# A two-layer trunk of RG-LRU and stick-breaking attention: three mask matmuls for four in each head, other shares of the last output tiles, and small moves in the half-wide unit

## The chip, the cores and the metric

The kernel runs on one core of a Trainium2 chip. The metric is the device time of one execution in microseconds (us); a kernel's time is the median of its runs. The trace was taken by the hardware profiler during one further execution, and that execution's own time is given beside its span.

Engines are named as the profile names them: PE is TensorE's matmuls, PEld its weight loads, DVE is VectorE, ACT is ScalarE, POOL is GpSimd, and SP is SyncE, which only issues transfers here.

## What is computed

The input is one sequence of 512 tokens with 1024 channels in float32. Two layers are applied, the first with an RG-LRU recurrent block, the second with stick-breaking attention of 16 heads of 64 channels; each is followed by a SwiGLU feed-forward network (FFN) of 2816 hidden channels, and a root-mean-square norm precedes each of the four. Cut to the parts that the change touches:

```python
def reference(x, norm_mix_g, norm_ffn_g, a_w_in, ...):
    for layer in range(DEPTH):
        h = _rmsnorm(x, norm_mix_g[layer])
        mix = rglru(h) if layer == 0 else _sb_mixer(h, b_w_qkv, b_w_out)
        x = x + mix
        h = _rmsnorm(x, norm_ffn_g[layer])
        x = x + (silu(h @ w_gate[layer]) * (h @ w_up[layer])) @ w_down[layer]
    return _rmsnorm(x, final_g)

def _stick_breaking_attention(q, k, v):           # one block of 128 queries
    z = (q @ k.T) / sqrt(64)
    mask = key_pos < q_pos                        # strictly causal
    log_beta = log_sigmoid(z)
    log_1m = where(mask, log_sigmoid(-z), 0.0)
    suffix = cumsum(log_1m, reverse=True) - log_1m
    wts = where(mask, exp(log_beta + suffix), 0.0)
    return wts @ v
```

## The kernel before, in words

**Precision.** Every float32 product is made of three fp32r matmuls: an operand is cast to a high part and the difference is its low part; `mm3` (L350) issues high by high, high by low, low by high (L352 to L354 in the trace). A weight tile of 128 x 1024 is loaded into `raw`, cast to `wh` (L306 on ACT, or L304 on DVE while `wh_dve` is set), and subtracted to `wl` (L307). `split_one` (L309) does this for the next tile in a fixed list, the plan. `wl_engine` (L321) chooses the engine of the subtraction: by the table `wl_on` (L191) for the tiles listed in it, else POOL for odd tiles and DVE for even ones outside the FFNs. Tiles 20 and 21 are the first two of the recurrent block's output weight `w_ao`.

**Order.** PE, ACT, DVE and POOL run their instructions in the order in which the program issues them in the FFNs and in attention, so the place of a call in the code is its place in each engine's queue. `chunk` (L329) hands out the next split weight tile and first splits ahead of it: the loop runs until `ahead` tiles beyond the one handed out are split, four in the FFNs, two elsewhere, unless an argument says otherwise.

**FFN.** The 2816 hidden channels are six units; units 0 to 4 are 512 channels wide and unit 5 (`u == NU`) 256. Each unit computes gate and up products for pairs of token blocks by seven products (`g1` to `g7`) instead of eight, and the down product in the same way (`d1` to `d7`), in an order given as a string (L56 to L64). For unit 5 it is

```python
self.order = "g5 g1 tt g6 o1 g3 o2 d1 g2 d2 g7 d6 d5 g4 q2 d7 tn d3 d4"
```

`product` (L846) takes one weight tile by `chunk` and issues its matmuls (L773 to L775 in the trace). `g3` adds bank results to the two tiles `u` (`u2_add`, L893, traced as L765). `q2` (L931) scales the two tiles `b` from two PSUM banks (L933). `tn` (L954) turns `u` and `b` by eight 128 x 128 transpositions (L780) into two banks.

**Attention.** Heads run in a software pipeline of 17 steps (L1275 to L1331). In step h, `s1(h+1)` (L1125) puts the scores of the next head into three PSUM banks: key block 0 with 512 queries in the first, key block 1 with 384 in the second, key blocks 2 and 3 with 256 and 128 in the third. Each key block takes two products (L1131, L1132) and one bf16 matmul of the identity with a mask tile (L1133), which adds −1e30 to the diagonal block of 128 columns. `chain_a` (L1138) forms softplus on ACT (Abs L1149, Exp L1150, Ln L1151), DVE and POOL; `s2` (L1175) adds the suffix sums by matmuls (L1186); `chain_b` (L1191) forms the weights' high and low parts (`awh`, `awl`, L1199 to L1201); `s3` (L1205, matmuls at L1212) multiplies them by v, and `s3_evac` (L1222) adds the result into `o` (L1225, L1226). After each second head `osplit` (L1242) forms the pair's high and low parts `oh` and `ol` (L1245, L1246).

While heads 0 to 12 run, PE has projections of later heads to fill its time. From step 13 on the fill is the output projection: `out_part(m, lo, hi)` (L1251) adds pairs lo to hi−1 into output tile m, three matmuls a pair. `out_split` splits one output weight tile with both the cast and the subtraction on DVE. Of the steps that matter here:

```python
elif h == 13: out_part(0, 0, 3, fill, 6)
elif h == 14: out_part(0, 3, 6, None, 6)
elif h == 15: osplit(6); out_part(1, 0, 6, fill)
elif h == 16: out_part(2, 0, 4, self.bank[0])
...
if h in (13, 15): out_split()        # behind s2(h) and chain_b(h), ahead of s3_evac(h - 1)
```

Behind the loop `osplit(7)` and the remaining parts of tiles 2, 1 and 0 follow.

Of the kernel before, what the change touches and what calls it, by code (L numbers as in the profile page):

```python
# [16 lines left out]
P = 128  # L17
# [153 lines left out]
class Kern:  # L171
    def __init__(self, ctx, tc, a, out):
        self.ctx, self.tc, self.nc, self.a, self.out = ctx, tc, tc.nc, a, out
        mk = lambda name, bufs, **kw: ctx.enter_context(tc.tile_pool(name=name, bufs=bufs, **kw))
        self.const = mk("const", 1)
        self.wp = mk("wp", 1)
        self.tp = mk("tp", 1)
        self.ar = mk("ar", 1)
        self.free = deque((0, i) for i in range(NS1))
        self.free2 = deque()  # L180
        self.clock = 0
        self.keep2 = 0
        self.slot = {}
        pp = mk("pp", 1, space=bass.MemoryType.PSUM)
        self.bank = [pp.tile([P, S], F32, name=f"bank{i}") for i in range(8)]
        self.bi = 0
        self.tn = 0
        self.later, self.done, self.chain = [], set(), {}
        self.wl_dve = self.wh_dve = False
        self.ring4 = None  # L190
        self.wl_on = {**dict.fromkeys((*range(5, 12), 14, 18), self.nc.gpsimd),  # L191
                      **dict.fromkeys((2, 3, 4, 12, 13, 15, 16, 17, 19), self.nc.vector)}
# [544 lines left out]
    def ffn(self, l, gnext):  # L737
# [3 lines left out]
        with tc.tile_pool(name=f"ffn{l}", bufs=1) as self.fp, \  # L741
# [96 lines left out]
            for u in range(NU + 1):  # L838
# [7 lines left out]
                def product(q, out, first=True):  # L846
                    for c in range(un.np):
                        wh, wl = self.chunk()
# [52 lines left out]
                def g3():  # L901
                    product(3, B, False)
                    u2_add()

# [49 lines left out]
                def tn():  # L954
                    turn((0, 1), A)
# [68 lines left out]
    def attention(self):  # L1024
# [5 lines left out]
        with ExitStack() as cx:  # L1030
# [6 lines left out]
            t0 = ap_.tile([P, P], F32, name="t0")  # L1037
# [3 lines left out]
            msk = ap_.tile([P, P], BF16, name="msk")  # L1041
            sp2 = [ap_.tile([P, S], F32, name="sp2")]
            for t in sp2:
# [8 lines left out]
            nc.gpsimd.affine_select(out=msk, in_=msk, compare_op=ALU.is_ge, fill=0.0,  # L1052
                                    base=0, pattern=[[-1, P]], channel_multiplier=1)
# [71 lines left out]
            def s1(h):  # L1125
                hd = heads[h]
                zt, b = zslot(h)
                for kt in range(4):
# [4 lines left out]
                    mm(zt[kt][:, 0:P], lhsT=idb, rhs=msk, start=False, stop=True, skip_group_check=True)  # L1133
# [95 lines left out]
            with tc.manual_schedule(engines={E.PE, E.Activation, E.DVE, E.Pool}):  # L1229
# [45 lines left out]
                for h in range(NH + 1):  # L1275
# [6 lines left out]
                    elif h == 13:  # L1282
                        fill = mps()
                        out_part(0, 0, 3, fill, 6)
                    elif h == 14:
                        out_part(0, 3, 6, None, 6)
# [3 lines left out]
                    elif h == 16:  # L1290
                        out_part(2, 0, 4, self.bank[0])
# [27 lines left out]
                    if h in (13, 15):  # L1319
# [9 lines left out]
                out_part(2, 4, 7)  # L1329
# [94 lines left out]
```

## Time and profile before

| | before |
|---|---|
| median of 3 runs | 1112.52 us (1112.18 to 1112.86) |
| the profiled execution's own time | 1113.21 us |
| its span in the trace | 1111.5 us, granted clock 0.997 |
| instructions | 14758 |
| DMA, mean over the span | 159.87 MB, 144 GB/s |
| mask matmuls (L1133) | 64, from 558.0 to 716.1 |

A row of the trace's timeline gives start, duration, engine, line, operation, out<-in with shapes, the count of instructions in the row, and in brackets the idle time of the engine before it and what ended it. Matmul ends are modelled and overlap the next start, so PE's pace is read from the distance of starts. A row of the windows gives the stretch, its length, then busy time and instructions of PE, PEld, DVE, ACT and POOL, then PE's granted clock, the DMA engines' share and GB/s. The lines themselves stand in the prediction.

### The profile page before, as it was taken

Reading aid. Unit: us, or ns where it says so; the run is one execution under the profiler, and the core shown is the slowest. Engines: PE = TensorE matmul, PEld = TensorE weight load, DVE = VectorE, ACT = ScalarE, POOL = GpSimd, SP = SyncE. Lnnn points to the kernel's source line nnn. Section 1 sums busy time; section 2 is a strip of 40 time slices with the busy share of each in tenths; the row PEclk is TensorE's granted clock in tenths of the full one; section 3 lists DMA queues with packets and bytes.
Section 4 is the critical chain, followed back from the end, with each engine's and each line's share of the span. In section 5 each row is a group of like instructions: output and inputs, shape, how many; then the busy total and the mean of one; then the engine's idle time right before and its main releaser. Section 6 shows DMA issues by size and latency. Waiting matters only on the chain.

```text
span 1111.5 us, 14758 instructions
## 1 busy us (share of the span) xinstructions
PE 1092.8 (98%) x5265; PEld 908.7 (82%) x5265; DVE 901.6 (81%) x1260; ACT 710.0 (64%) x1084; POOL 359.9 (32%) x251
## 2 busy tenths in 40 slices
PE   9999999999999999999999999999999999999996
PEld 6888788878888888888888888778888888888885
DVE  7878887687978888987378889968669797978897
ACT  7598567565646464535389999957765555646454
POOL 2353242324151413204043445403232424151411
PEclk9999999999999999999999999999999999999999
DMA  8512339877667765442243423224987766765421
GB/s 284 172 71 99 112 109 214 189 199 183 161 193 157 197 164 171 99 130 94 84 121 96 117 77 95 77 76 125 212 180 204 169 188 168 164 193 119 149 63 75
DMA packets 48825, 159.87 MB, mean 144 GB/s; under 512 B 6000, under 2 KB 7280, under 8 KB 48752
## 3 DMA queue, kind: packets, MB, share of 16 engines
q1 hardware_dynamic: 36368, 113.84, 29.7%
q0 software_dynamic: 12384, 45.09, 23.2%
q8 instruction: 41, 0.67, 0.2%
q14 instruction: 32, 0.26, 0.1%
HBM read 148.43 MB, written 2.10 MB: 135 GB/s over the span
## 4 chain that ended last, share of the span: by engine, by line
PE 76%; DVE 9%; ACT 3%; issue 2%; DMA 1%; POOL 0%; DVEq 0%; ACTq 0%; POOLq 0%
PE bank L773 16%; PE bank L774 16%; PE bank L775 16%; PE bank L352 7%; PE bank L354 7%; PE bank L353 7%; DVE wl L307 4%; PE bank L1186 3%; PE bank L1212 2%; DVE y L765 1%; PE bank L780 1%; DMA bu<-w_gu 1%; PE bank L1131 1%; ACT wh L306 1%; PE bank L1132 1%
## 5 line engine op out<-in xcount | busy, mean ns | idle before, releaser
L307 DVE TENSOR_TENSOR wl<-raw,wh 128x1024 fp32r<-128x1024 f32 (+1 forms) x117 | 176.4, 1511 | 37.6 <-ACT wh L306 37.4
L306 ACT CAST wh<-raw 128x1024 fp32r<-128x1024 f32 (+1 forms) x142 | 143.1, 1012 | 91.9 <-PE bank L775 38.2
L773 PE MATMUL bank<-wh,ow 128*128 128x512 f32 (+1 forms) x480 | 179.8, 375 | 1.8 <-DVE u L765 1.8
L775 PE MATMUL bank<-wh,ow 128*128 128x512 f32 (+1 forms) x480 | 178.3, 372 | 0.0
L774 PE MATMUL bank<-wl,ow 128*128 128x512 f32 (+1 forms) x480 | 178.3, 371 | 0.0
L92 POOL DMA_DIRECT2D bu<-w_gu x64 | 56.0, 876 | 270.0 <-DVE wl L307 101.4
L306 ACT CAST wh<-bu 128x1024 fp32r<-128x1024 f32 x66 | 69.4, 1053 | 65.7 <-PE bank L775 40.5
L307 DVE TENSOR_TENSOR wl<-bu,wh 128x1024 fp32r<-128x1024 f32 x66 | 80.5, 1237 | 32.6 <-ACT wh L306 31.6
L773 PEld LDWEIGHTS bank<-wh,ow 128*128 128x128 f32 x480 | 90.4, 188 | 18.3 <-DVE u L765 2.6
L775 PEld LDWEIGHTS bank<-wh,ow 128*128 128x128 f32 x480 | 90.4, 188 | 15.7
L352 PE MATMUL bank<-uh,wh 128*128 128x512 f32 x256 | 102.3, 400 | 0.8 <-ACT uh L408 0.8
L774 PEld LDWEIGHTS bank<-wl,ow 128*128 128x128 f32 x480 | 90.4, 188 | 15.4
L354 PE MATMUL bank<-uh,wl 128*128 128x512 f32 x256 | 100.1, 392 | 0.4 <-DVE wl L307 0.4
L353 PE MATMUL bank<-ul,wh 128*128 128x512 f32 x256 | 99.7, 389 | 0.3 <-DVE ul L409 0.3
L307 POOL TENSOR_TENSOR wl<-raw,wh 128x1024 fp32r<-128x1024 f32 (+1 forms) x27 | 62.1, 2301 | 101.9 <-ACT wh L306 99.4
L765 DVE TENSOR_TENSOR y<-y,bank 128x512 f32<-128x512 f32 x140 | 88.9, 679 | 2.4 <-PE bank L775 2.3
L773 PE MATMUL bank<-wh,hth 128*128 128x512 f32 x192 | 75.2, 392 | 0.1
L774 PE MATMUL bank<-wl,hth 128*128 128x512 f32 x192 | 74.8, 389 | 0.0
L775 PE MATMUL bank<-wh,htl 128*128 128x512 f32 x192 | 74.7, 389 | 0.0
L307 DVE TENSOR_TENSOR wl<-bv,wh 128x1024 fp32r<-128x1024 f32 x44 | 58.3, 1336 | 13.2 <-ACT wh L306 13.2
L1154 POOL TENSOR_TENSOR spl<-t,sph 128x512 fp32r<-128x512 f32 (+1 forms) x32 | 39.1, 1244 | 84.1 <-DVE sph L1153 81.2
L306 ACT CAST wh<-bv 128x1024 fp32r<-128x1024 f32 x44 | 46.0, 1051 | 18.1 <-PE bank L775 8.7
(258 smaller groups left out, 2778.0 us busy)
## 6 DMA issues: line engine op xcount, KB each, us to landing
bu<-w_gu POOLq DMA_DIRECT2D x64, 512.0 KB, 5.8
raw<-w_gu SPq DMA_DIRECT2D x44, 512.0 KB, 3.8
raw<-w_dn SPq DMA_DIRECT2D x24, 512.0 KB, 5.3
bu<-w_gu SPq DMA_DIRECT2D x22, 512.0 KB, 4.2
bv<-w_gu SPq DMA_DIRECT2D x22, 512.0 KB, 4.3
bv<-w_gu POOLq DMA_DIRECT2D x22, 512.0 KB, 6.2
d<-w_dn SPq DMA_DIRECT2D x20, 512.0 KB, 3.5
raw<-w_qk SPq DMA_DIRECT2D x16, 512.0 KB, 3.4
```

Of the source, the lines that this page charges most:

```text
L92: kern.soon(lambda: kern.nc.gpsimd.dma_start(t, self.part(n), accum_op=ALU.add))
L306: self.nc.scalar.copy(wh[:, c], raw[:, c])
L307: self.wl_engine(i).tensor_tensor(wl[:, c], raw[:, c], wh[:, c].bitcast(F32), ALU.subtract)
L352: mm(out, lhsT=wh, rhs=xh, start=first, stop=False)
L353: mm(out, lhsT=wh, rhs=xl, start=False, stop=False)
L354: mm(out, lhsT=wl, rhs=xh, start=False, stop=last)
L765: add = lambda o, a, b: nc.vector.tensor_tensor(o, a, b, ALU.add)
L773: mm(out, lhsT=xh, rhs=wh, start=first, stop=False, skip_group_check=True)
L774: mm(out, lhsT=xh, rhs=wl, start=False, stop=False, skip_group_check=True)
L775: mm(out, lhsT=xl, rhs=wh, start=False, stop=last, skip_group_check=True)
L1154: nc.gpsimd.tensor_tensor(sl[:, w], sp[:, w], sh[:, w].bitcast(F32), ALU.subtract)
L1186: mm(zt[kt][:, o0:o0 + ZW[j]], lhsT=tri if j == kt else one_n, rhs=s_, start=False, stop=True, skip_group_check=True)
```

## The change

- `wl_on`: tile 20's subtraction goes to POOL (tile 21's was there by the default).
- Unit 5, `g3`: `chunk(3)` splits one tile fewer ahead of g3's products; that split comes by `split_one` behind the adds of `u2_add`.
- Unit 5, `tn`: the same eight transpositions, first the four of `u`, then the four of `b`. Before, the first four went into bank 2 (two of `u`, two of `b`) and the others into bank 3; now the third and fourth turn `u` into bank 3.
- Masks: key block 0's mask stays behind its products. Those of key blocks 1 to 3 stand behind all products of the head: one of 128 columns in the second bank, one of 256 columns in the third. `msk` is 256 columns wide, made by two `affine_select` on POOL.
- Output tiles: of tile 0, step 13 does two pairs (three before) and step 14 four; of tile 2, step 16 does pairs 0 to 4 (0 to 3 before) and the tail 5 and 6.
- `out_split` of output weight tile 2 stands in step 14, not 15.
- `t0` is a temporary of the ring of six instead of a tile of its own.

```diff
--- before.py
+++ after.py
@@ -188,7 +188,7 @@
         self.later, self.done, self.chain = [], set(), {}
         self.wl_dve = self.wh_dve = False
         self.ring4 = None
-        self.wl_on = {**dict.fromkeys((*range(5, 12), 14, 18), self.nc.gpsimd),
+        self.wl_on = {**dict.fromkeys((*range(5, 12), 14, 18, 20, 21), self.nc.gpsimd),
                       **dict.fromkeys((2, 3, 4, 12, 13, 15, 16, 17, 19), self.nc.vector)}
 
     def ps(self):
@@ -845,7 +845,7 @@
 
                 def product(q, out, first=True):
                     for c in range(un.np):
-                        wh, wl = self.chunk()
+                        wh, wl = self.chunk(3 if u == NU and q == 3 else None)
                         for j in range(2):
                             for i in range(un.kt):
                                 k = c * un.kt + i
@@ -901,6 +901,8 @@
                 def g3():
                     product(3, B, False)
                     u2_add()
+                    if u == NU:
+                        self.split_one()
 
                 G = B4
 
@@ -952,7 +954,11 @@
                     operands2(1, db, self.cx)
 
                 def tn():
-                    turn((0, 1), A)
+                    for ab in (u2, b5):
+                        for f in range(2):
+                            for j in range(2):
+                                t = j + 2 * (ab is b5)
+                                nc.tensor.transpose(A[f][:, ts(t)], ab[j][:, ts(f)], self.ident)
                     for p in range(2):
                         split([t[:, p] for t in hn], A[p])
 
@@ -1034,11 +1040,11 @@
             vs = [[None] * 4 for _ in range(NT)]
             o = [None] * NP
             ou = [None] * NP
-            t0 = ap_.tile([P, P], F32, name="t0")
+            t0 = self.tmp()[:, :P]
             tri = ap_.tile([P, P], F32R, name="tri")
             one_n = ap_.tile([P, P], F32R, name="one_n")
             idb = ap_.tile([P, P], BF16, name="idb")
-            msk = ap_.tile([P, P], BF16, name="msk")
+            msk = ap_.tile([P, 2 * P], BF16, name="msk")
             sp2 = [ap_.tile([P, S], F32, name="sp2")]
             for t in sp2:
                 nc.vector.memset(t[:, 0:P], 0.0)
@@ -1049,8 +1055,9 @@
             nc.vector.tensor_copy(tri, t0)
             nc.vector.tensor_copy(idb, self.ident)
             nc.gpsimd.memset(msk, NEG)
-            nc.gpsimd.affine_select(out=msk, in_=msk, compare_op=ALU.is_ge, fill=0.0,
-                                    base=0, pattern=[[-1, P]], channel_multiplier=1)
+            for i in range(2):
+                nc.gpsimd.affine_select(out=msk[:, ts(i)], in_=msk[:, ts(i)], compare_op=ALU.is_ge, fill=0.0,
+                                        base=0, pattern=[[-1, P]], channel_multiplier=1)
             zb = self.bank[:6]
             mb = list(self.bank[6:])
             self.mi = 0
@@ -1125,12 +1132,15 @@
             def s1(h):
                 hd = heads[h]
                 zt, b = zslot(h)
+                masks = {0: ((0, 0, P),), 3: ((1, 0, P), (2, P, 3 * P))}
                 for kt in range(4):
                     qs = slice(QO[kt], S)
                     lk = hd["ks"][:, ts(kt)]
                     mm(zt[kt], lhsT=lk, rhs=hd["qh"][:, qs], start=kt < 3, stop=False, skip_group_check=True)
                     mm(zt[kt], lhsT=lk, rhs=hd["ql"][:, qs], start=False, stop=False, skip_group_check=True)
-                    mm(zt[kt][:, 0:P], lhsT=idb, rhs=msk, start=False, stop=True, skip_group_check=True)
+                    for i, lo, hi in masks.get(kt, ()):
+                        mm(b[i][:, lo:hi], lhsT=idb, rhs=msk[:, :hi - lo], start=False, stop=True,
+                           skip_group_check=True)
                 self.rel(hd["qh"], hd["ql"], hd["ks"])
 
             BR = (slice(0, 512), slice(0, 384), slice(128, 512))
@@ -1281,14 +1291,14 @@
                             proj_evac1(t)
                     elif h == 13:
                         fill = mps()
-                        out_part(0, 0, 3, fill, 6)
+                        out_part(0, 0, 2, fill, 6)
                     elif h == 14:
-                        out_part(0, 3, 6, None, 6)
+                        out_part(0, 2, 6, None, 6)
                     elif h == 15:
                         osplit(6)
                         out_part(1, 0, 6, fill)
                     elif h == 16:
-                        out_part(2, 0, 4, self.bank[0])
+                        out_part(2, 0, 5, self.bank[0])
                     if h + 1 < NH:
                         s1(h + 1)
                         if h == 14:
@@ -1316,7 +1326,7 @@
                         chain_b(h)
                     if h == 15:
                         s3(h - 1)
-                    if h in (13, 15):
+                    if h in (13, 14):
                         out_split()
                     if h >= 1:
                         s3_evac(h - 1)
@@ -1326,7 +1336,7 @@
                         due = nsp
                         nsp += 1
                 osplit(7)
-                out_part(2, 4, 7)
+                out_part(2, 5, 7)
                 out_part(1, 6, 7)
                 out_part(0, 6, 7, self.bank[1])
             for m in range(3):
```

On DVE at the end of steps 14 and 15 (banks are numbered 70 to 77; L1226 is head 13's add into `o`, `ol` is `osplit(6)`, the last three rows are the low parts of head 15), before:

```order
L1165 CAST r_752_6615<-t_6614 128x256
L1201 TENSOR_TENSOR awl_6624<-bank_72,awh_6623 128x384
L1167 TENSOR_TENSOR r_752_6615<-t_6614,r_752_6615 128x256
L1226 TENSOR_TENSOR o_6490<-bank_76,t_6629 64x512
L1246 TENSOR_TENSOR ol_6633<-o_6490,oh_6632 128x512
L1201 TENSOR_TENSOR awl_6673<-bank_73,awh_6672 128x512
L1201 TENSOR_TENSOR awl_6678<-bank_74,awh_6677 128x384
L1201 TENSOR_TENSOR awl_6683<-bank_75,awh_6682 128x384
```

and now, with the same lines ten to the right in number (L1167 is L1177, L1226 is L1236, L1246 is L1256):

```order
L1175 CAST r_753_6600<-t_6599 128x256
L1211 TENSOR_TENSOR awl_6609<-bank_72,awh_6608 128x384
L1177 TENSOR_TENSOR r_753_6600<-t_6599,r_753_6600 128x256
L304 CAST wh_6614<-raw_6154 128x1024
L307 TENSOR_TENSOR wl_6615<-raw_6154,wh_6614 128x1024
L1236 TENSOR_TENSOR o_6473<-bank_76,t_6618 64x512
L1256 TENSOR_TENSOR ol_6622<-o_6473,oh_6621 128x512
L1211 TENSOR_TENSOR awl_6662<-bank_73,awh_6661 128x512
L1211 TENSOR_TENSOR awl_6667<-bank_74,awh_6666 128x384
L1211 TENSOR_TENSOR awl_6672<-bank_75,awh_6671 128x384
```

The cast and the subtraction of output weight tile 2 now stand ahead of head 13's add, of `ol` and of head 15's low parts.

On DVE in unit 5 of the first FFN, behind the low part `hal` that d1 uses (`u` are the two tiles of `u2_add`, `wl` is the weight tile of d2), before:

```order
L764 TENSOR_TENSOR hal<-t_3758,hah 128x256
L307 TENSOR_TENSOR wl_3763<-raw_3541,wh_3762 128x1024
L765 TENSOR_TENSOR u_1495<-u_1495,bank_70 128x256
L765 TENSOR_TENSOR u_1496<-u_1496,bank_71 128x256
L765 TENSOR_TENSOR t_3794<-t_3758,bank_75 128x256
```

and now:

```order
L764 TENSOR_TENSOR hal<-t_3758,hah 128x256
L765 TENSOR_TENSOR u_1495<-u_1495,bank_70 128x256
L765 TENSOR_TENSOR u_1496<-u_1496,bank_71 128x256
L307 TENSOR_TENSOR wl_3789<-raw_3541,wh_3788 128x1024
L765 TENSOR_TENSOR t_3792<-t_3758,bank_75 128x256
```

The two adds into `u` have moved ahead of the subtraction.

On PE in one head's `s1` (banks 70 to 72 are the three score banks, `idb` the identity in bf16), from the second key block on, before:

```order
L1132 MATMUL bank_71<-ql_4956,ks_5048 128x384
L1133 LDWEIGHTS idb
L1133 MATMUL bank_71<-msk,idb 128x128
L1131 MATMUL bank_72<-qh_4955,ks_5048 128x256
L1132 MATMUL bank_72<-ql_4956,ks_5048 128x256
L1133 LDWEIGHTS idb
L1133 MATMUL bank_72<-msk,idb 128x128
L1131 MATMUL bank_72<-qh_4955,ks_5048 128x128
L1132 MATMUL bank_72<-ql_4956,ks_5048 128x128
L1133 LDWEIGHTS idb
L1133 MATMUL bank_72<-msk,idb 128x128
L352 MATMUL bank_77<-uh_4211,wh_4967 128x512
```

and now (L1139 and L1140 are the products, L1142 the mask):

```order
L1139 MATMUL bank_71<-qh_4953,ks_5045 128x384
L1140 MATMUL bank_71<-ql_4954,ks_5045 128x384
L1139 MATMUL bank_72<-qh_4953,ks_5045 128x256
L1140 MATMUL bank_72<-ql_4954,ks_5045 128x256
L1139 MATMUL bank_72<-qh_4953,ks_5045 128x128
L1140 MATMUL bank_72<-ql_4954,ks_5045 128x128
L1142 LDWEIGHTS idb
L1142 MATMUL bank_71<-msk,idb 128x128
L1142 LDWEIGHTS idb
L1142 MATMUL bank_72<-msk,idb 128x256
L352 MATMUL bank_77<-uh_4211,wh_4965 128x512
```

Two masks between products are gone; a mask of 128 and one of 256 columns stand behind the last product, ahead of the projection's matmuls.

## The prediction

> **What bounds the kernel now.** I read the busy times first, then TensorE's (PE's) waits, then windows of the stages that the change touches, and last the rows around each place.
>
> ```profile
> PE 1092.8 (98%) x5265; PEld 908.7 (82%) x5265; DVE 901.6 (81%) x1260; ACT 710.0 (64%) x1084; POOL 359.9 (32%) x251
> PE bank L354 <- DVE wl L307: 2.0, 3, 1.1
> 580.00:600.00 20.00, 20.00 (x111) 16.52 (x110) 17.71 (x31) 19.25 (x38) 9.57 (x8) 1.00 0.38 107
> 728.00:732.00 4.00, 2.03 (x9) 1.35 (x8) 3.49 (x5) 1.30 (x3) 0.00 (x0) 0.97 0.02 4
> 732.00:736.00 4.00, 4.00 (x13) 3.17 (x13) 0.00 (x0) 0.00 (x0) 0.00 (x0) 0.60 0.36 131
> ```
>
> The first row gives each engine's busy time: PE works 98% of the span, so a microsecond is saved only where PE issues less, waits less, or runs at a better clock. The next is one of PE's waits (for whom: us in all, times, longest); the change touches two of its three. The last three are windows (length, then busy time and instructions of PE, PEld, DVE, ACT, POOL, then PE's granted clock). Among the heads, at 580 to 600, PE is never idle, with ACT close behind at 19.25 of 20. At 728 to 732 PE stands idle for half the time, and in the 4 us behind it runs at a granted clock of 0.60. That is the largest loss that the change can reach.
>
> **The change part by part.** All times are of the one profiled execution, which took 1113.21 us (span 1111.5); the three runs have their median at 1112.52, 0.69 below it. I subtract from the former and move the result by 0.69.
>
> *The weight split before the last two heads (out_split, out_part).*
>
> ```profile
> 723.87 0.68 DVE L1226 TENSOR_TENSOR o<-bank,t 64x512 f32<-64x512 f32 x1
> 724.59 0.62 ACT L1245 CAST oh<-o 128x512 fp32r<-128x512 f32 x1 [1.53 <-DVE o L1226]
> 726.05 0.60 ACT L1199 ACTIVATE awh<-bank 128x512 fp32r<-128x512 f32 x1 [0.84 <-PE bank L1186]
> 727.08 0.80 PE L1212 MATMUL bank<-awh,vs 128*128 128x512 f32 x4
> 727.72 0.80 PE L1212 MATMUL bank<-awl,vs 128*128 128x512 f32 x4
> 729.23 0.68 DVE L304 CAST wh<-raw 128x1024 fp32r<-128x1024 f32 x1
> 729.94 1.23 DVE L307 TENSOR_TENSOR wl<-raw,wh 128x1024 fp32r<-128x1024 f32 x1
> 729.96 0.50 PE L352 MATMUL bank<-oh,wh 128*128 128x512 f32 x1 [1.44 <-DVE wh L304]
> 731.20 0.33 SPq L287 DMA_DIRECT2D raw<-w_bo  x1
> 731.22 0.51 PE L354 MATMUL bank<-oh,wl 128*128 128x512 f32 x1 [0.53 <-DVE wl L307]
> 735.20 0.77 PE L1212 MATMUL bank<-awh,vs 128*128 128x512 f32 x4
> 736.43 0.44 PE L352 MATMUL bank<-oh,wh 128*128 128x512 f32 x1
> 738.62 0.69 DVE L1246 TENSOR_TENSOR ol<-o,oh 128x512 fp32r<-128x512 f32 x1 [0.69 <-ACT oh L1245]
> 739.90 0.39 PE L352 MATMUL bank<-oh,wh 128*128 128x512 f32 x1
> ```
>
> PE has issued s3(14) by 728.36 (its second four begin 0.64 behind its first, so they are through another 0.64 on). It then waits 1.44 for the cast of output weight tile 2 and 0.53 for its wl; the slow clock follows, and s3(15) starts at 735.20. Twelve products stood between. At full clock fifteen take 739.90 − 736.43 = 3.47, or 0.231 each. In the changed kernel cast and wl stand on DVE where the o add of 723.87 stands now: ready by 723.87 + 0.68 + 1.23 = 725.8, before PE asks. Fifteen products, not twelve, then stand ahead of s3(15): it starts at 728.36 + 3.47 = 731.83, 3.37 earlier, and three products fewer (0.69) are left behind it. Sum: **−4.1**. The split also frees its raw buffer for the next load (SP's 731.20, issued when wl was done), which then comes 5.4 earlier and can only help.
>
> What is late next? The o add of head 13 moves by 1.91 to end at 726.45; s3(14) wants its bank at 727.08, a slack of 0.6. On ACT the cast oh waits for that add and stands ahead of the exponentials of head 15 (726.05 now), so that they begin at 726.45 + 0.62 = 727.07, 1.0 later; their last awl would come to about 730.45 and head 14's o add to 731.15, both before 731.83. At the tail ol of pair 7 is ready 739.31 − 735.20 = 4.11 behind the start of s3(15); PE asks for it 1.23 (s3) + 13 × 0.231 = 4.23 behind, so that it just fits. If these slacks fail, half of the gain is my bound: −2.0 to −4.2.
>
> The other three moved products (tile 0, ahead of s1(15) instead of s1(14)):
>
> ```profile
> 706.36 0.60 ACT L1149 ACTIVATE t<-bank 128x512 f32<-128x512 f32 x1 [0.26 <-PE bank L1133]
> 714.80 0.44 PE L1131 MATMUL bank<-qh,ks 128*128 128x384 f32 x1 [0.40 <-DVE awl L1201]
> ```
>
> ACT waited 0.26 there for the mask of s1(14), so that head's chain starts up to 0.26 earlier; the 0.68 of products then stands where PE waits 0.40 for DVE, which hides part of it. I take **−0.25**, bounds 0 and −0.68.
>
> *The wl of weight tile 20 goes from DVE to POOL (wl_on).*
>
> ```profile
> 114.22 1.05 ACT L306 CAST wh<-raw 128x1024 fp32r<-128x1024 f32 x1
> 117.76 2.41 POOL L307 TENSOR_TENSOR wl<-raw,wh 128x1024 fp32r<-128x1024 f32 x1 [9.78 <-ACT wh L306]
> 118.40 2.85 DVE L307 TENSOR_TENSOR wl<-raw,wh 128x1024 fp32r<-128x1024 f32 x1
> 119.84 0.39 PE L353 MATMUL bank<-al,wh 128*128 128x512 f32 x1
> 121.30 0.50 PE L354 MATMUL bank<-ah,wl 128*128 128x512 f32 x1 [1.07 <-DVE wl L307]
> 121.64 0.40 PE L352 MATMUL bank<-ah,wh 128*128 128x512 f32 x1
> ```
>
> This wl took 2.85 on DVE, beside POOL's 2.41, where the row at 729.94 has 1.23 for the same shape; PE waited for it. POOL has been idle for 9.78 and can begin when the cast is done, at 115.3: 115.3 + 2.4 = 117.7, and the next tile's wl then runs to 120.1 as before. From L353 to the next L352 PE spent 121.64 − 119.84 = 1.80 where two products cost 0.46: **−1.34**. The bounds are that and 0, the latter if the time is lost again in the recurrent block behind it.
>
> *Unit 5 (g3, then tn), once in each of the two FFNs.*
>
> ```profile
> 1063.50 1.23 DVE L307 TENSOR_TENSOR wl<-raw,wh 128x1024 fp32r<-128x1024 f32 x1 [0.52 <-ACT wh L306]
> 1064.64 0.75 DVE L765 TENSOR_TENSOR u<-u,bank 128x256 f32<-128x256 f32 x2
> 1065.11 0.39 PE L773 MATMUL bank<-wh,ow 128*128 128x256 f32 x1 [0.87 <-DVE u L765]
> 1085.60 0.44 PE L780 MATMUL bank<-ident,u 128*128 128x128 f32 x2 [0.37 <-DVE b L933]
> 1086.16 0.38 PE L780 MATMUL bank<-ident,u 128*128 128x128 f32 x2
> ```
>
> DVE stood 0.52 for ACT's cast with two u adds (0.75) queued behind the wl, and PE waited 0.87 for the adds. With the adds ahead of the wl, they run in the 0.52, and PE goes on about 1.04 earlier. But from there to its line 933, 20 us later, DVE has no pause, and PE waits for L933 again (the 0.37 at 1085.60): what lasts is what DVE gains, 0.52. Bounds 0 and −1.04, the whole of the gain; I take −0.52, twice: **−1.04**. In tn the eight turns take 1086.16 − 1085.60 = 0.56 for the first four, 0.14 each. L933 comes twice, and its second instruction reads bank 3 and writes the last b. So far the fourth turn was the first to need it (for that b); now the third is (u into bank 3). PE meets the same wait one turn sooner, and has one turn more left behind it: it can't gain, and loses 0.14 at most. I take +0.1, twice: **+0.2**.
>
> *Masks: three matmuls for four, over the same 512 columns, each head.*
>
> ```profile
> L1133 PE MATMUL bank<-msk,idb x64: 229/230/233, 558.0 to 716.1; 128*128 128x128 bf16 x64
> 619.68 0.33 PE L1132 MATMUL bank<-ql,ks 128*128 128x384 f32 x1
> 619.85 0.10 PEld L1133 LDWEIGHTS <-idb 128*128 128x128 bf16 x1 [0.15 <-issue]
> 619.85 0.23 PE L1133 MATMUL bank<-msk,idb 128*128 128x128 bf16 x1
> 620.09 0.28 PE L1132 MATMUL bank<-ql,ks 128*128 128x256 f32 x1
> 620.40 0.27 PE L1132 MATMUL bank<-ql,ks 128*128 128x128 f32 x1
> 620.51 0.23 PE L1133 MATMUL bank<-msk,idb 128*128 128x128 bf16 x1
> ```
>
> From L1132 (384 columns) to the next L1132 at 620.09, 0.41 pass; the first product takes 0.17 until the mask, and the 256 columns of the next by that rate 0.11, so that the mask costs 0.13. From 620.09 to 620.40 the third costs, in the same way, 0.31 − 0.11 − 0.11 (the last as from 620.40 to the mask at 620.51) = 0.09. Both go: −0.22. What comes: behind the last product a second mask, of 256 columns, with its own load of idb. No row has it; its bounds are 0.10, about the cheapest mask, and 0.24, as a mask of 0.13 whose further 128 columns cost as much as fp32r columns in this place (0.11). I take 0.17, near the 0.13 of an ordinary mask and a little wider: −0.05 a head, for fifteen heads **−0.75**; bounds +0.3 and −1.8. The second affine_select and the new place of t0 I cost at nothing: they stand ahead of the heads, and the first mask isn't wanted until 558.0; without that cover they would cost some tenths.
>
> [...]
>
> The sum is −4.1 − 0.25 − 1.34 − 1.04 + 0.2 − 0.75 = −7.3: 1113.21 − 7.3 = 1105.9, and 0.69 less in the median: **1105.2**.
>
> **The rivals.** *The split crowds head 14's chain* (10%): o, oh or awl come late and PE waits in another place. For it: slacks of 0.6 and less. Against: each slack was worked out with DVE and ACT in the new order, and none is below zero. The term is then −2.0: 1107.3.
>
> *The slow clock stays* (6%): a half-speed stretch follows some other pause. For it: the 0.60 behind PE's pause at 728. Against: the pause is what goes. At a clock of 0.60, 4 us lose 4 × 0.40 = 1.6: 1106.8. [...]
>
> *Masks bring nothing* (10%): 1106.0. *DVE's pause in unit 5 was covered by something else* (8%): 1106.2. *Both adds' gain is kept whole* (8%): 1104.2.
>
> *Slower* (3%): masks of banks 1 and 2 now end with the whole of s1, and ACT's Abs of bank 1 waits for them.
>
> ```profile
> 621.64 0.48 ACT L1149 ACTIVATE t<-bank 128x384 f32<-128x384 f32 x1
> ```
>
> That Abs comes at 621.64; its mask, now through by about 620.1, would be through by 620.85. The slack is 0.8. Where ACT comes earlier than the mask, each head's chain waits, and ACT, busy 19.25 of 20, has no room to regain it: 0.75 × 14 heads = 10.5 less the other gains of 6.5: +4, 1116.5. It decides from the point where Abs finds its bank unready. *The change does little of what it says* (4%), each wait only moving to the next: 1111.5.
>
> **How the numbers follow.** My forecast has 51%, the rivals the rest. The range holds the bounds of the sum, though not all at one end: with the masks, unit 5 and tn at their good ends 1105.2 − 1.05 − 1.0 − 0.3 = 1102.8, and with the out term at −2.0, the masks at +0.3 and half of tile 20's gain 1105.2 + 2.1 + 1.0 + 0.7 = 1109.0. A measurement of this kernel can tell about 0.2% (2.2 us) from no change. Faster by more than that 0.93, within it 0.04, slower 0.03.
>
> **What would show it right or wrong.** In the profile of the changed kernel: no wait of L352 or L354 for the cast and wl of output tile 2, and no granted clock below 0.9 in the 4 us windows behind it; s3(15) some 3.4 earlier against s3(14). No wait of L354 near 120. DVE's u adds ahead of the wl in unit 5, and PE's wait at the turns of 0.4 or more. PE in the heads 0.05 shorter from one s1 to the next. It would be wrong if PE waits for o or awl in heads 14 to 16, if ACT waits for mask rows in the middle heads, or if a half-speed stretch turns up elsewhere.

## The result, and the profile after

The changed kernel takes 1106.76 us (median of 6 runs, 1105.82 to 1109.07) where the kernel before, measured beside it again, takes 1112.69: a ratio of 0.9941, with a 95% interval of 0.9925 to 0.9957. A second measurement on another occasion (experiment e11) gave 0.9940 (0.9926 to 0.9954). One execution of e1 took 1823.46 us at a mean granted clock of 0.556, and e1's ratio leaves it out. The forecast was 1105.2 with a range of 1102.8 to 1109.0. The profiled execution took 1106.96 and has a span of 1105.3, 6.2 below the span before.

From the page and the waits of the changed kernel, and its windows behind the place where the slow clock was:

```profile
PE 1089.0 (99%) x5249; PEld 907.2 (82%) x5249; DVE 901.4 (82%) x1259; ACT 709.8 (64%) x1084; POOL 363.2 (33%) x253
PE bank L1139 <- DVE awl L1211: 1.5, 3, 0.7
PE bank L773 <- DVE y L765: 1.0, 2, 0.5
PE bank L961 <- DVE b L935: 0.7, 2, 0.3
PE bank L354 <- DVE wl L307: 0.3, 1, 0.3
728.00:732.00 4.00, 4.00 (x21) 3.41 (x21) 1.35 (x3) 1.36 (x3) 0.00 (x0) 1.00 0.01 4
732.00:736.00 4.00, 4.00 (x20) 3.18 (x19) 2.34 (x4) 1.94 (x4) 0.00 (x0) 1.00 0.00 0
```

The waits for tile 20's wl, for output tile 2's wh and wl, and for the u adds are gone. PE's pause at 728 and the clock of 0.60 behind it are gone too: both windows are full at 1.00. Two waits are new, and the forecast had neither: 1.5 for awl in three heads (L1139 is the old L1131), where the kernel before waited 0.4 in one head (0.7 of it is the piece of chance told below), and 1.0 for the y adds, half of it in unit 5 of either FFN.

To see where the time went, the same PE instruction was taken from both traces, and its start in the kernel before subtracted from its start here. The shift then changes only where the kernels differ, or where an execution differs from another one. Each number of this table is how much PE's shift grew across a stretch (negative is earlier), against the one profiled execution of the kernel before:

| stretch, by the times of before | forecast | changed | changed again (e11) |
|---|---|---|---|
| start to 109.6 | 0 | +0.80 | +2.06 |
| 109.6 to 121.6, tile 20 | −1.34 | −1.35 | −1.35 |
| 217.9 to 242.2, start of the first FFN | 0 | +0.09 | −0.86 |
| 447.0 to 555.5, unit 5 of the first FFN | −0.42 | −0.31 | −0.30 |
| 555.5 to s3(14), the heads | −1.0 | −0.97 | −1.15 |
| s3(14) to 742.2, the last output tiles | −4.1 | −4.00 | −4.00 |
| 1055.6 to 1091.8, unit 5 of the second FFN | −0.42 | −0.53 | −0.50 |

The first and the third row are not the change's: across all traces of this study, the first goes from −0.54 to +2.06 and the third from −0.87 to +2.13, in kernels with and without the change. PE waits there for the first normalized inputs (`uh` on ACT: 0.8 in the kernel before and in the changed one, 1.2 in e11; `ul` on DVE: 0.3 in the first two) and, at the start of the FFN, for DVE's operands (`hbl`: 0.2 in the kernel before, 0.4 in the changed one). A part of the two largest shifts at the start is the clock: in e11 it is granted at 0.50 from 9.0 to 12.4, in e5 (+1.88) from 9.5 to 12.9, where the kernel before has 1.00. What makes the rest differ between executions was not settled; by these traces such starts are a large part of what executions differ by.

### The profile page after: what moved, and what is told of

Read it like the earlier page. It is cut to its first block, busy times and chain, and to the rows that moved or that the text cites. A ratio compares the mean times of both kernels' runs of the same rounds, so it can differ in the third digit from the quotient of the medians.

```text
span 1105.3 us, 14729 instructions
## 1 busy us (share of the span) xinstructions
PE 1089.0 (99%) x5249; PEld 907.2 (82%) x5249; DVE 901.4 (82%) x1259; ACT 709.8 (64%) x1084; POOL 363.2 (33%) x253
## 4 chain that ended last, share of the span: by engine, by line
PE 69%; DVE 10%; ACT 6%; issue 4%; DMA 2%; POOL 0%; DVEq 0%; POOLq 0%; ACTq 0%
PE bank L773 15%; PE bank L774 15%; PE bank L775 15%; PE bank L352 6%; PE bank L354 6%; PE bank L353 6%; DVE wl L307 3%; PE bank L1196 2%; DMA bu<-w_gu 2%; PE bank L1222 1%; DVE y L765 1%; ACT wh L306 1%; PE bank L780 1%; ACT t L1160 1%; ACT t L1159 1%
## 5 line engine op out<-in xcount | busy, mean ns | idle before, releaser
L307 DVE TENSOR_TENSOR wl<-raw,wh 128x1024 fp32r<-128x1024 f32 (+1 forms) x116 | 172.1, 1487 | 36.1 <-ACT wh L306 36.0
```

The source lines that it names most:

```text
L307: self.wl_engine(i).tensor_tensor(wl[:, c], raw[:, c], wh[:, c].bitcast(F32), ALU.subtract)
```

## The experiments

All were run beside the kernel before. "Shift" is PE's shift as above; the whole row of shifts for the heads and behind them stands at the end of this section.

### e1: the masks alone

```diff
 (before)
+masks = {0: ((0, 0, P),), 3: ((1, 0, P), (2, P, 3 * P))}
-mm(zt[kt][:, 0:P], lhsT=idb, rhs=msk, ...)
+for i, lo, hi in masks.get(kt, ()):
+    mm(b[i][:, lo:hi], lhsT=idb, rhs=msk[:, :hi - lo], ...)
```

> The kernel before with the mask part alone (three mask matmuls for four, t0 as a temporary). Theory: each steady head is 0.19 us shorter on PE (0.12 and 0.08 for the two removed masks, and the 256-column mask as good as free), until PE catches up with the chain of ACT and DVE that frees its score banks (DVE's awl); from there heads alternate and gain little. So about 1.0 to 1.8 us are left at the last s3, depending on whether DVE's subtraction of r (128x256) meets POOL's wl in the second head and takes 2.6 us instead of 0.4. Rival (the forecast's own figure): 0.05 a head, 0.75 in all, no limit by the chain. Rival: nothing in steady heads, since weight loads are hidden: 0.

Ratio 0.9981 (0.9968 to 0.9995). Shift over the heads −1.17. From one s3 to the next, heads 3 to 7 are 0.19 or 0.20 shorter each, heads 1 and 2 not at all, and of heads 8 to 13 every second one (8, 10 and 12) is 0.10 to 0.17 longer than before, the others 0.15 to 0.19 shorter. This is the first theory; the forecast's 0.05 a head falls, and so does 0. In the kernel before the load of a product starts with the matmul ahead of it (L1132's at 618.93, its own matmul at 619.15); the load of idb starts with its own mask (both at 619.38, and both at 619.85).

The masks at the end of a steady head of the changed kernel, beside the rows of before in the prediction:

```profile
618.49 0.23 PE L1142 MATMUL bank<-msk,idb 128*128 128x128 bf16 x1
618.53 0.42 PE L1139 MATMUL bank<-qh,ks 128*128 128x384 f32 x1
618.79 0.33 PE L1140 MATMUL bank<-ql,ks 128*128 128x384 f32 x1
618.96 0.28 PE L1139 MATMUL bank<-qh,ks 128*128 128x256 f32 x1
619.19 0.22 PE L1139 MATMUL bank<-qh,ks 128*128 128x128 f32 x1
619.25 0.28 PE L1140 MATMUL bank<-ql,ks 128*128 128x128 f32 x1
619.37 0.34 PE L1142 MATMUL bank<-msk,idb 128*128 128x128 bf16 x2
619.47 0.47 PE L352 MATMUL bank<-uh,wh 128*128 128x512 f32 x1
```

A lone mask holds its place for 0.04 (618.49 to 618.53), and the product behind it then takes 0.26 where the next of the same size takes 0.17. Two masks in a row take 0.09 to 0.10 together, so the second adds 0.05 to 0.06, 256 columns though it has; the slow product behind comes once for both (0.31 to the next product, as behind the single mask before). The forecast had 0.17 for it. The first product of 128 columns, with no mask ahead of it, takes 0.06 (619.19 to 619.25), where the forecast had 0.11. So the mask that stood there cost 0.13 and not 0.09, and the head gains 0.13 twice less 0.06, about the 0.19 to 0.20 seen.

### e2: the changed kernel with the masks of before

```diff
 (changed)
-masks = {0: ((0, 0, P),), 3: ((1, 0, P), (2, P, 3 * P))}
+mm(zt[kt][:, 0:P], lhsT=idb, rhs=msk, ...)     # behind each key block
```

> The changed kernel with the masks of before (one behind each key block). Theory: PE's place at the start of the last heads is that of the changed kernel less what the masks brought, about 1.0 us later; no wait of PE for awl in the second and third head; everything else as in the changed kernel, the 3.9 us around the last heads above all. Total about 1.0 us above the changed kernel. Rival: the waits for awl come from the other parts (the earlier start after tile 20 and unit 5), then they stay, and the total is the same as the changed kernel's or lower.

Ratio 0.9950 (0.9934 to 0.9967). Shift over the heads −0.13, no wait for awl in heads 1 and 2, last output tiles −4.00 as with the change. In the heads the first theory held: the waits for awl belong to the masks. In the total it did not show: the median of 1106.72 is that of the changed kernel, and both intervals are some 3.5 us wide. The profiled spans hide it too (1105.0 against 1105.3), because this execution lost nothing at the start of the first FFN where the changed kernel's lost 0.95 (−0.86 against +0.09).

### e3: g3 alone

```diff
 (before)
-wh, wl = self.chunk()
+wh, wl = self.chunk(3 if u == NU and q == 3 else None)
 ...
 u2_add()
+if u == NU:
+    self.split_one()
```

> The kernel before with the reordering in g3 alone. Theory: in each FFN PE's products behind u2_add start about 1.0 us earlier, and 0.5 of it is left at the turns of tn, where PE waits for DVE's scaling of b (L933 there); 1.0 in all at the end, and PE's new wait ahead of it is for DVE's y adds. Rival: all of the 1.0 is kept, 2 us in all. Rival: none is kept.

One run, 1110.39. In the first FFN PE's shift is −1.11 behind the adds and −0.54 at 555.5; in the second −1.25 and −0.71. Half is kept, as expected. The other half goes into the wait of 0.5 for the y adds, 9 us ahead of the turns and in both FFNs, which the kernel before does not have. DVE is busy from the adds to the turns (20.97 of the 21.00 us from 1058 to 1079 in the changed kernel). DVE's rows in the second FFN of the changed kernel show the adds where DVE's 0.52 of waiting was:

```profile
1056.80 0.42 DVE L764 TENSOR_TENSOR hal<-t,hah 128x256 fp32r<-128x256 f32 x1 [0.23 <-ACT hah L769]
1057.14 0.74 DVE L765 TENSOR_TENSOR u<-u,bank 128x256 f32<-128x256 f32 x2
1057.81 1.22 DVE L307 TENSOR_TENSOR wl<-raw,wh 128x1024 fp32r<-128x1024 f32 x1
```

This kernel also shows something else. It has the same pauses at the last output tiles as the kernel before, but not the slow clock:

```profile
729.39 0.50 PE L352 MATMUL bank<-oh,wh 128*128 128x512 f32 x1 [1.44 <-DVE wh L304]
730.65 0.50 PE L354 MATMUL bank<-oh,wl 128*128 128x512 f32 x1 [0.53 <-DVE wl L307]
728.00:731.00 3.00, 1.08 (x4) 0.60 (x5) 2.78 (x4) 0.73 (x2) 0.00 (x0) 1.00 0.02 5
731.00:735.00 4.00, 4.00 (x21) 3.43 (x20) 0.19 (x1) 0.53 (x1) 0.00 (x0) 1.00 0.40 131
```

1.44 and 0.53 to the hundredth, and then 1.00 where the kernel before had 0.60 and e1, with the same pauses, 0.57 (both at 0.50 for the same 3.4 us, 731.8 to 735.2 and 731.2 to 734.6; the means of 4 us differ by where they are laid). The shift across the last output tiles is −1.58 here with nothing changed in them. So 1.6 of the 4.0 is a loss that the kernel before meets in some executions (two of these three) and not in others. The length of a pause alone does not decide it here: e6 falls to 0.50 behind a wait of 1.08, and e7 stays at 1.00 behind one of 2.35. What does was not settled.

### e4: the changed kernel with the turns of tn in the old order

```diff
 (changed)
-for ab in (u2, b5): ... nc.tensor.transpose(A[f][:, ts(t)], ab[j][:, ts(f)], self.ident)
+turn((0, 1), A)
```

> The changed kernel with the turns of tn in the old order. Theory: PE leaves the turns 0.1 us earlier in each FFN than in the changed kernel, 0.2 in all, which no timing can show and the trace can: the distance from the first turn to the first product behind the eight falls from about 1.05 to 0.92. Rival: the new order is the faster one, and the distance grows.

One run, 1105.93. The turns in this kernel, then in the changed one:

```profile
1078.31 0.44 PE L780 MATMUL bank<-ident,u 128*128 128x128 f32 x2 [0.33 <-DVE b L935]
1078.59 0.45 PE L780 MATMUL bank<-ident,b 128*128 128x128 f32 x2
1079.22 0.47 PE L773 MATMUL bank<-wh,hth 128*128 128x512 f32 x1
```

```profile
1079.22 0.83 PE L961 MATMUL bank<-ident,u 128*128 128x128 f32 x4 [0.32 <-DVE b L935]
1079.89 0.60 PE L961 MATMUL bank<-ident,b 128*128 128x128 f32 x4
1080.25 0.47 PE L773 MATMUL bank<-wh,hth 128*128 128x512 f32 x1
```

From the first turn to the product behind them 0.91 against 1.03: the new order costs 0.12 a time, as forecast. By shifts, unit 5 brings −0.40 and −0.78 here, −0.31 and −0.53 with the new order.

### e5 and e8: the split in step 14, without and with the share of tile 2

```diff
 (before)
-if h in (13, 15):
+if h in (13, 14):
     out_split()
 (e8 also)
-out_part(2, 0, 4, self.bank[0])
+out_part(2, 0, 5, self.bank[0])
-out_part(2, 4, 7)
+out_part(2, 5, 7)
```

> The kernel before with out_split in step 14 alone, the output tiles' shares as before. Theory: the waits of PE for wh and wl of output tile 2 (1.44 and 0.53) go, PE has no pause and so no slow clock behind it, and s3(15) starts 12 products behind s3(14): 728.4 + 2.8 = 731.1 against 735.2 in the kernel before, 4.0 earlier where the kernel before meets the slow clock and 2.4 where not. But ol of pair 7 is ready 4.1 behind the start of s3(15) while PE has its 12 + 3 products of the tail in 4.9: no wait there, so the share of tile 2 is worth nothing by itself. Rival (the forecast's reason for moving a pair ahead of s3(15)): with 12 products s3(15) comes before head 14's o add or head 15's awl, and PE waits for them by 0.3 or more; then this kernel loses that against the changed one.

> The kernel before with out_split in step 14 and the share of tile 2 (five pairs ahead of s3(15), two in the tail), tile 0 as before. Theory: from s3(14) to the last product of the tail the same as with the split alone within 0.1, and as in the changed kernel; what tile 0's share brings is the rest, 0.1 at s3(13). Rival: the share is worth 0.3 or more against the split alone.

One run each: 1113.32 and 1110.74, which tells nothing, since the shifts at 242 are +4.03 and +1.11 already. Across the last output tiles the shifts are −4.00 and −3.99: the split alone does it all, and the share of tile 2 is worth nothing. Of s3(15) alone, e5 brings it 4.03 earlier and e8 3.34, the difference being the three products of the fifth pair. e5's windows behind s3(14):

```profile
728.00:732.00 4.00, 4.00 (x26) 3.70 (x25) 3.14 (x4) 1.43 (x3) 0.00 (x0) 1.00 0.27 87
732.00:736.00 4.00, 4.00 (x21) 3.27 (x21) 2.49 (x4) 2.44 (x6) 0.00 (x0) 1.00 0.12 48
```

Tile 0's share is the difference at s3(14) between e2 and these two: −0.13 in the heads of e2, −0.03 and +0.02 here, so about 0.1.

### e6: all three masks behind the last product

```diff
 (changed)
-masks = {0: ((0, 0, P),), 3: ((1, 0, P), (2, P, 3 * P))}
+masks = {3: ((0, 0, P), (1, 0, P), (2, P, 3 * P))}
```

> The changed kernel with all three masks behind the last product of each head, the first key block's too. Theory: a mask costs PE what the change of weights around it costs, and masks that follow each other cost next to nothing, so each steady head is another 0.1 shorter on PE; but ACT's Abs of the first bank, which starts 0.15 behind its mask so far, then waits for the end of the head's products, 1.0 later, and the chain of ACT, which sets the pace from head 8 on, hands this to PE: no gain or a loss, up to 0.5 a head, 5 in all. Rival: PE alone sets the pace, then 1.5 less than in the changed kernel.

One run, 1112.56; shift over the heads +5.66. From one s3 to the next PE gains 0.26 in odd heads from 3 to 11 and loses 0.36 to 0.79 in even ones from 4 to 12, 1.12 in head 1 and 1.26 in head 13; it waits 4.0 for awl, six times. ACT shows the cause in its waits over the heads, one of which is shown as a row, and the last row is a window behind PE's wait of 1.08 for awl (until 706.01):

```profile
618.13 1.05 ACT L306 CAST wh<-raw 128x1024 fp32r<-128x1024 f32 x1
619.64 0.60 ACT L1159 ACTIVATE t<-bank 128x512 f32<-128x512 f32 x1 [0.46 <-PE bank L1142]
ACT t L1159 <- PE bank L1142: 9.8, 14, 1.5
708.00:712.00 4.00, 4.00 (x17) 3.31 (x17) 2.05 (x4) 3.61 (x7) 0.31 (x1) 0.57 0.02 4
```

ACT stands for the mask that now comes last 14 times, 9.8 in all, where in the changed kernel it is 0.5, and can't make it up. A part of the loss, up to 4 × 0.43 = 1.7, is the clock of 0.57. This is the slower rival of the prediction, on the first bank; on the second and third bank, where the changed kernel moves the masks, ACT comes late enough.

### e7: the split of k late

```diff
 (changed)
-if t < 16 and t % 2:            # ahead of s2(h) and chain_b(h)
-    proj_evac2(t)
 ...
-if t < 16 and t % 2 == 0:       # behind s3_evac(h - 1)
+if t < 16:
     proj_evac2(t)
```

> The changed kernel with proj_evac2 of the k tiles behind s3_evac, as that of the q tiles stands, so that the 2.1 us of DVE for ks and 1.3 us of ACT no longer stand ahead of awl in every second head. Theory: the awl chain caps what the masks gain (PE waits for awl in heads 1, 2 and every second one from 8 on); without the cap each of some 13 heads is 0.19 shorter than in the kernel before, about 2.6 at the last s3 where the changed kernel has 1.0: 1.2 to 1.8 us less than the changed kernel. Rival: the cap is ACT's 95% of busy time, or POOL's hold on DVE, and the total stays. Rival: ks now come too late for s1 and PE waits: slower.

Ratio 1.0009 (0.9997 to 1.0021), 0.7% above the changed kernel: the last rival. PE waits for ks itself now, and hardly for awl (the waits in the heads):

```profile
PE bank L1139 <- DVE ks L1125: 9.1, 7, 2.4
PE bank L1139 <- DVE awl L1211: 0.4, 1, 0.4
```

The heads between are 0.19 shorter as always. The edit took a need of the next head away along with the cap, so it could not tell whether the cap is ks and awl by themselves.

### e9, e10, e11, e12: what caps the heads

In the changed kernel awl of steps 8, 10 and 12 comes late for the s1 that follows. In steps 8 and 10 `osplit` of a finished pair stands on ACT and DVE ahead of ks and awl. DVE of the changed kernel there, with the first product of s1 in each of the three banks:

```profile
655.28 0.89 DVE L1256 TENSOR_TENSOR ol<-o,oh 128x512 fp32r<-128x512 f32 x1
656.10 0.68 DVE L1103 SCALAR_TENSOR_TENSOR t<-bank,acc 128x512 f32<-128x512 f32 x1
657.73 2.11 DVE L1125 TENSOR_TENSOR ks<-t,ks 64x512 fp32r<-64x512 f32 x2
659.88 0.69 DVE L1211 TENSOR_TENSOR awl<-bank,awh 128x512 fp32r<-128x512 f32 x1
660.62 0.50 PE L1139 MATMUL bank<-qh,ks 128*128 128x512 f32 x1
660.82 0.55 DVE L1211 TENSOR_TENSOR awl<-bank,awh 128x384 fp32r<-128x384 f32 x1
661.42 0.44 PE L1139 MATMUL bank<-qh,ks 128*128 128x384 f32 x1
661.48 0.55 DVE L1211 TENSOR_TENSOR awl<-bank,awh 128x384 fp32r<-128x384 f32 x1
662.09 0.39 PE L1139 MATMUL bank<-qh,ks 128*128 128x256 f32 x1
664.48 0.69 DVE L1162 SCALAR_TENSOR_TENSOR t<-bank,t 128x512 f32<-128x512 f32 x1 [1.40 <-issue]
```

The three awl end at 660.57, 661.37 and 662.03, and each bank's first product starts 0.05 or 0.06 behind: PE takes each bank as soon as awl lets it go, though no row shows PE idle, since the ends are modelled. This s1 takes 2.08 (660.62 to 662.70) where the one of the head ahead takes 1.44. In the kernel before it took 1.98, so the cap was there already. DVE idles 1.40 later on. e9 moves `osplit` to the end of the step; e10 has the old turns besides; e11 is the changed kernel again; e12 moves only the first four pairs.

```diff
 (changed)
-due = nsp                       # osplit(due) in the middle of the next step
+osplit(nsp)                     # e9, e10
+if nsp < 4: osplit(nsp)         # e12
+else: due = nsp
```

> The changed kernel with osplit of a finished pair at the end of its step, behind s3_evac, not in the middle of the next step ahead of proj_evac2 and awl. Theory: from head 8 on PE waits in every second head for awl, because oh (0.6 on ACT) and ol (0.9 on DVE) stand ahead of ks and awl there; DVE has 1.4 us to spare at the step's end. Without them in the way heads 8, 10 and 12 are 0.19 shorter, as heads 3 to 7 are, and not 0.1 longer: 0.6 to 0.9 less at the last s3 than in the changed kernel. Rival: ks and awl alone set that cap, and the last s3 comes as in the changed kernel within 0.2.

> The same with the turns of tn in the old order. Theory: 0.6 to 0.9 from the heads and 0.1 to 0.2 from each tn against the changed kernel, about 1.1 us in all, less than its runs scatter by (the start alone scatters by 2); so the trace must show it. Rival: as the changed kernel.

> The changed kernel once more beside the two, on the same chip. Theory: 0.5% to 0.6% below the kernel before, with the same shifts in its trace from tile 20, g3, the heads and the output tiles, and another shift at the first 13 us and at the start of the first FFN. Rival: the shift of 0.8 at the start belongs to the change, then it is there again.

e9 0.9969 (0.9956 to 0.9982), e10 0.9969 (0.9958 to 0.9981), e11 0.9940 (0.9926 to 0.9954): the first two are 0.3% worse than the changed kernel. Both sides are in the trace. Heads 8 and 10 are now 0.13 shorter than before, not 0.1 longer, where the theory has 0.19. But from step 10 on PE loses up to 1.6 a head. There the pair is split in the step that finishes it, and on ACT its cast stands for DVE's add (e9):

```profile
686.02 0.62 ACT L1255 CAST oh<-o 128x512 fp32r<-128x512 f32 x1 [1.78 <-DVE o L1236]
706.16 0.50 PE L1139 MATMUL bank<-qh,ks 128*128 128x512 f32 x1 [1.08 <-DVE awl L1211]
```

ACT loses 1.78, and PE pays for it in the heads that follow. e12 leaves these two pairs where they were:

> The changed kernel with osplit at the end of the step for the first four pairs alone, and the turns of tn in the old order. Theory: with pairs 4 and 5 at the end of the step that has just finished them, oh stood on ACT behind head 9's or 11's o add (1.8 idle) and the chain came late: that goes with them, and heads 11 to 13 are as in the changed kernel again; heads 8 and 10 stay about 0.13 shorter than in the kernel before, not 0.1 longer: 0.4 to 0.5 less at the last s3 than in the changed kernel, and 0.2 to 0.3 from the turns. 0.7 in all, which the trace shows and the total may not. Rival: the late heads lose again, since the loss came from the freed tiles or from PE being ahead.

Ratio 0.9929 (0.9915 to 0.9942), median 1106.75. The shift over the heads is −1.63, against −0.97 and −1.15 in the two profiles of the changed kernel, and unit 5 brings −0.42 and −0.73: 0.5 to 0.7 and 0.3 better in the trace, as expected. The times themselves don't tell it from the changed kernel, whose interval overlaps.

### The shifts side by side

| kernel | heads | last output tiles | unit 5, first and second FFN |
|---|---|---|---|
| changed | −0.97 | −4.00 | −0.31, −0.53 |
| changed again (e11) | −1.15 | −4.00 | −0.30, −0.50 |
| e1 masks alone | −1.17 | −0.02 | +0.09, −0.19 |
| e2 changed, old masks | −0.13 | −4.00 | −0.28, −0.60 |
| e3 g3 alone | 0.00 | −1.58 | −0.54, −0.71 |
| e4 changed, old turns | −1.15 | −4.00 | −0.40, −0.78 |
| e5 split alone | −0.03 | −4.00 | +0.13, −0.11 |
| e6 all masks last | +5.66 | −3.89 | −0.29, −0.55 |
| e7 k split late | +6.28 | −4.00 | −0.27, −0.61 |
| e8 split and share | +0.02 | −3.99 | +0.07, −0.12 |
| e9 osplit at the end | +1.56 | −3.98 | −0.26, −0.58 |
| e10 and old turns | +1.59 | −4.00 | −0.43, −0.78 |
| e12 first four pairs | −1.63 | −4.00 | −0.42, −0.73 |

Rows without an edit in a column show its scatter: 0.03 in the heads, about 0.1 to 0.2 in the second FFN.

## Why the prediction was right, and where it was not

The direction, the range and the largest term were right, and the total came within 1.6 us (0.14%). That it came so close is in part luck, since two errors in the masks offset each other. Point by point:

- **The weight split.** Forecast −4.1, measured −4.00 in every trace that has it, with the mechanism as described: the waits gone, no pause, no slow clock. The slacks held: s3(14) starts without a wait, head 15's exponentials moved by 1.3 against head 14's products and their awl still came in time. DVE and ACT of the changed kernel show the queue that was worked out:

```profile
722.32 0.68 DVE L304 CAST wh<-raw 128x1024 fp32r<-128x1024 f32 x1
723.03 1.22 DVE L307 TENSOR_TENSOR wl<-raw,wh 128x1024 fp32r<-128x1024 f32 x1
724.28 0.68 DVE L1236 TENSOR_TENSOR o<-bank,t 64x512 f32<-64x512 f32 x1
725.00 0.62 ACT L1255 CAST oh<-o 128x512 fp32r<-128x512 f32 x1 [3.40 <-DVE o L1236]
725.34 0.80 PE L1222 MATMUL bank<-awh,vs 128*128 128x512 f32 x4
728.95 0.68 DVE L1236 TENSOR_TENSOR o<-bank,t 64x512 f32<-64x512 f32 x1
730.11 0.74 PE L1222 MATMUL bank<-awh,vs 128*128 128x512 f32 x4
```

  What the step left out is that 1.6 of it is the clock's, which the kernel before loses only in some executions; in the others the term is 2.4 (−4.00 less e3's −1.58). Against a median of many runs it is therefore somewhat less than against the one profile that the forecast was worked out on. The share of tile 2, which the working carried along, is worth nothing (e5 and e8).
- **Tile 20.** Forecast −1.34, measured −1.34 or −1.35 in each of the traces with it, and −0.02 to −0.05 in those without.
- **Unit 5.** g3's −0.52 a time measured −0.40 and −0.54 in the first FFN (e4, e3), −0.71 and −0.78 in the second, of which about 0.15 is scatter. The turns' +0.1 measured 0.12. That DVE is the bound held, but the place of the wait did not: the forecast wanted a wait of 0.4 or more at the turns, and it is 0.32 there (0.37 before); the half that is lost goes into the new wait of 0.5 for the y adds, 9 us earlier.
- **Masks.** The sum, −0.75, is near the −0.9 to −1.2 measured, but two steps behind it failed and offset each other. The price of the 256-column mask was put at 0.17 and is 0.05 to 0.06, and that of the third mask at 0.09 and is 0.13, so that a steady head gains 0.19 and not 0.05; and all fifteen heads were counted as bounded by PE, where only those from 3 to 7 and every second one later are. In the others the gain goes into waits for awl. The windows shown before, with ACT at 19.25 of 20, pointed there; the forecast used that row for one rival and not for the sum. e12 shows that part of this cap is `osplit`'s place. What sets the rest stays open, since e7 could not tell.
- **Tile 0's share.** Forecast −0.25, measured about −0.1.

The forecast's sum of −7.3 stands against −7.0 in the trace when the start's +0.8, which is scatter, is set aside. Of the rivals, that the masks bring nothing fell (e1), and so did the crowding of head 14's chain. The slow clock that stays fell for the changed kernel (neither of its two traces has it in the heads or behind them). It is not gone from every kernel with the early split: in e6, where PE waits longer for awl, a stretch at 0.50 stands at 708.1 to 711.5. Half of g3's gain was kept, not all and not none.

One piece of chance should not be read as the change's. In the second step of the heads, DVE's subtraction of r and POOL's wl of a weight tile start within 0.04 of each other. Kernel before, then the changed one:

```profile
578.43 2.70 POOL L307 TENSOR_TENSOR wl<-raw,wh 128x1024 fp32r<-128x1024 f32 x1 [2.63 <-ACT wh L306]
578.46 0.42 DVE L1167 TENSOR_TENSOR r<-t,r 128x256 fp32r<-128x256 f32 x1
```

```profile
577.67 2.40 POOL L307 TENSOR_TENSOR wl<-raw,wh 128x1024 fp32r<-128x1024 f32 x1 [2.62 <-ACT wh L306]
577.71 2.65 DVE L1177 TENSOR_TENSOR r<-t,r 128x256 fp32r<-128x256 f32 x1
586.28 0.44 PE L1139 MATMUL bank<-qh,ks 128*128 128x384 f32 x1 [0.70 <-DVE awl L1211]
```

POOL's lead is 0.04 here and 0.03 in the kernel before (0.031 and 0.028 to the nanosecond). Here POOL's goes first by the durations, DVE's 0.42 becomes 2.65, and PE waits 0.70. In e1, e2, e4, e11 and e12 the lead is 0.01 to 0.03 and DVE's goes first. One execution alone went the other way, so that the lead decides it is not shown. The head behind gave most of it back: the shift goes from −0.83 to −0.01 and back to −0.70. Where POOL's goes first, DVE's ends 0.29 behind it (580.36 and 580.07); where DVE's goes first, POOL's is longer by 0.30 (2.70 against 2.40). Why either takes longer beside the other is not shown by these traces.

## What to carry to other kernels

- When PE is 98% busy, look for the place where it is idle and at a low clock, and ask which split, cast or load stands too late on another engine: putting one of 1.9 us a step earlier was the largest single part of this change, 2.4 us, and 4.0 where the slow clock would have followed.
- A gain on PE in a repeated step lasted here only until PE met the next engine's chain: with the masks alone heads 3 to 7 kept 0.19 to 0.20 each, and heads 8, 10 and 12 took 0.10 to 0.17 more than before (e1), so the sum over steps needs the other engine's slack as well as PE's price.
- Where single executions scatter by more than the term that is asked for, shifts of the same instruction between two traces tell terms of 0.1 us that the times can't.

## What the runs showed of the hardware that was not expected

- Equal pauses of PE (1.44 and 0.53) were followed by a granted clock of 0.50 for 3.4 us in two executions and of 1.00 in a third; a wait of 1.08 in e6 was followed by 0.50 for 3.4 us, one of 2.35 in e7 by 1.00.
- A bf16 mask between fp32r products costs PE 0.13, most of it (0.09) as a slow product behind it; a second mask right behind the first, with its own load of the same weights and 256 columns, 0.05 to 0.06.
- DVE's subtraction of r and POOL's of a wl, which start some 0.03 us apart, went one way in one execution and the other way in the others: DVE's took 2.65 in the one, 0.42 in the kernel before.
